# State-space steps of a hybrid block: inputs scaled once, whole-tile products with ScalarE placing the halves, one scan per tile

## The chip, the cores and the metric

The kernel runs on one core of a Trainium2 chip. The core has a matrix engine (TensorE, PE in the tables), a vector engine (VectorE, DVE), a scalar engine (ScalarE, ACT), a general engine (GpSimd, POOL) and a queue engine (SyncE, SP) that only issues transfers. They run side by side and wait for one another by semaphores; each takes its own instructions strictly in the order in which they were placed. The metric is the device time of one launch in microseconds (us).

## The reference, cut to what matters

The whole program is two transformer-like blocks, each with a mixture of experts. The change lies in one part of the first block, the state-space mix of 512 channels in 32 groups of 16, with 64 complex states for each group, over a sequence of 1024, once forwards and once backwards:

```python
def _ssm_direction(ug, a_re, a_im, log_dt, b_re, b_im, c_re, c_im, reverse):
    lam = lax.complex(a_re, a_im)
    dt = jnp.exp(log_dt)[:, None]
    a_bar = jnp.exp(lam * dt)
    b_bar = ((a_bar - 1.0) / lam)[..., None] * b_mat      # input matrix, scaled
    bu = jnp.einsum('blgc,gnc->blgn', ug, b_bar)
    _, h = lax.associative_scan(_scan_combine, (a, bu), axis=1, reverse=reverse)
    return jnp.einsum('blgn,gcn->blgc', h, c_mat).real

y = _ssm_direction(..., False) + _ssm_direction(..., True)
y = y + d_skip * u
```

In the same block 20 column blocks of a projection (`h @ w_in`, four for the Fourier part and 16 for the gates) don't depend on the state-space part.

## The kernel before, in words

The stage in question is the middle of `phase_a`. Two generators are run together there. `gates` has 20 column blocks of 128; each loads 512 KB of weights, splits them into a high and a low part (`split_hi_lo`: ScalarE copies the high part `sh`, line 55; VectorE subtracts for the low part `sl`, line 61), and multiplies twice 24 products of 128x512 into the PSUM tile `psg` (lines 210 to 212, helper `fm_block`; 960 products in all). ScalarE takes each finished `psg` into `go` (line 339). `ssm_steps` is the other one. The sequence of 1024 is cut into 128 blocks of 8 positions, the 32 groups into 4 lots `b`, with 2 directions `d`: 8 steps. What the two loops set is only the order in the program text. A list scheduler then fixes the order of the instructions on each engine when the program is built, with estimated durations; it places the rest of the program too.

A step has four pieces, and piece after piece is emitted a loop turn later than the one before, so that neighbouring steps overlap:
- `params1` scales the input matrix (`bbr`, `bbi`, a complex product `cmul` of 64 columns, lines 149 to 154), multiplies it with powers of the decay into `ptr` and `pti` (`cmul`, 512 columns), turns the output matrix by four products on TensorE (line 564, into `ct`), builds the block-diagonal `cbd` on GpSimd (lines 568 to 572), and forms `q`, whose real part stands in partitions 0 to 63 and whose imaginary part in 64 to 127 (lines 580 to 589). In `ptr` and the other parameter tiles the two halves of the partitions are instead two groups of channels, so real and imaginary results have to be placed half by half.
- `params2` builds rotation tables `ec`, `es` on GpSimd, and turns `ptr` and `pti` on TensorE (line 606), copied out by ScalarE into `pres` and `pims` (line 607). `ug_make` turns the inputs into `ug` (lines 623, 624).
- `scan` multiplies `ug` with `pres` and `pims` (line 634), rotates the result (lines 642 to 647, with two of the six operations on GpSimd), runs the recurrence as eight scans of 128 columns (line 651), rotates back (lines 661 to 667), and places the result in `st` by halves (lines 665, 670).
- `r_make` and `y_out` move a small convolution block through memory and form the output (lines 710, 712).

Ahead of the stage, `phase_a` reads and normalizes `x`, and projects the state-space inputs `us` (line 320 copies them out). `ssm_params` forms the decay powers, and loads `b_re`, `b_im`, `c_re`, `c_im`. A third generator, `ada_steps` (lines 1361 to 1388), forms a modulation vector out of large weights `w_ada`: 8 parts of it run beside the projection of `us`, and one goes with each call of `gates` from the 21st on. The rest of the program (the gated unit and the Fourier part, the first mixture of experts, the second block) follows in order.

Of the kernel before, what the change touches and what calls it, by code (L numbers as in the profile page):

```python
# [13 lines left out]
AF = mybir.ActivationFunctionType  # L14
OP = mybir.AluOpType
AX = mybir.AxisListType
P = 128
# [10 lines left out]
class Core:  # L28
# [6 lines left out]
    def sb(self, pool, shape, dt=FT, tag=None, bufs=None):  # L35
        self.n += 1
        kw = {"name": f"{tag or 't'}_{self.n}"}
        kw["tag"] = tag or kw["name"]
        if bufs is not None:
            kw["bufs"] = bufs  # L40
        return pool.tile(shape, dt, **kw)


def bcast(ap, shape):
    return ap.to_broadcast(shape)
# [102 lines left out]
def cmul(E, o_re, o_im, a_re, a_im, b_re, b_im, t1, t2):  # L148
    E.tensor_tensor(t1, a_re, b_re, op=OP.mult)
    E.tensor_tensor(t2, a_im, b_im, op=OP.mult)  # L150
    E.tensor_tensor(o_re, t1, t2, op=OP.subtract)
    E.tensor_tensor(t1, a_re, b_im, op=OP.mult)
    E.tensor_tensor(t2, a_im, b_re, op=OP.mult)
    E.tensor_tensor(o_im, t1, t2, op=OP.add)
# [275 lines left out]
def ssm_params(k, keep, pool, prm, T):  # L430
    nc = k.nc
    V, G, A, PE = nc.vector, nc.gpsimd, nc.scalar, nc.tensor
    sb = k.sb
# [8 lines left out]
    t1 = sb(pool, sh, tag="t1")  # L442
    t2 = sb(pool, sh, tag="t2")
# [24 lines left out]
    f_re = sb(keep, sh, tag="fre")  # L468
# [52 lines left out]
    for nm in ("re", "im"):  # L521
        tb["b_" + nm] = sb(keep, [P, 2, 16, 16], tag="b_" + nm)
        tb["c_" + nm] = sb(keep, [P, 2, 4, 64], tag="c_" + nm)
        for d in range(2):
            nc.sync.dma_start(out=tb["b_" + nm][:, d], in_=T["ssm_B_" + nm][0, d].rearrange("(q g) n c -> (g n) q c", g=2))
            nc.sync.dma_start(out=tb["c_" + nm][:, d],
                              in_=T["ssm_C_" + nm][0, d].rearrange("(b g) c n -> (g c) b n", b=4))
    return dict(**tb, pw_re=pw_re, pw_im=pw_im, f_re=f_re, f_im=f_im, r8=r8, er=er)


def ssm_steps(k, jit, pp, pr, us, ident, kd_d, T):
# [3 lines left out]

    def params1(b, d):
        br, bi = [pr[n][:, d, 4 * b:4 * b + 4] for n in ("b_re", "b_im")]
# [11 lines left out]
        b_re = sb(jit, [P, 4, 16], tag="bbr")  # L549
        b_im = sb(jit, [P, 4, 16], tag="bbi")  # L550
        fr = bcast(pr["f_re"][:, cols].unsqueeze(2), [P, 4, 16])
        fi = bcast(pr["f_im"][:, cols].unsqueeze(2), [P, 4, 16])
        cmul(V, b_re, b_im, br, bi, fr, fi, t1[:, :, 0, :], t2[:, :, 0, :])
# [7 lines left out]
        for g in range(2):  # L561
            pg = slice(64 * g, 64 * g + 64)
            for a, n in enumerate(("c_re", "c_im")):
                PE.matmul(ctp[pg, a * P:(a + 1) * P], pr[n][:, d, b, :], ident, start=True, stop=True)
            A.activation(ct[pg], ctp[pg, 0:256].rearrange("p (a q g c) -> p a q g c", a=2, q=4, g=2)[:, :, :, g, :],
                         AF.Copy)
        cbd = sb(jit, [P, 2, 4, 2, 16], tag="cbd")
        G.memset(cbd, 0.0)
        for g in range(2):
            pg = slice(64 * g, 64 * g + 64)  # L570
            G.tensor_copy(cbd[pg, 0, :, g, :], ct[pg, 0])
            G.tensor_scalar(cbd[pg, 1, :, g, :], ct[pg, 1], -1.0, None, op0=OP.mult)
# [5 lines left out]
        t1 = sb(jit, [P, 4, 8, 16], tag="p1")  # L578
        t2 = sb(jit, [P, 4, 8, 16], tag="p2")
        V.tensor_tensor(t1, cre, pre, op=OP.mult)  # L580
        V.tensor_tensor(t2, cim, pim, op=OP.mult)
        for g in range(2):
            pg = slice(64 * g, 64 * g + 64)
            V.tensor_tensor(q[0:64, :, g], t1[pg], t2[pg], op=OP.subtract)
        V.tensor_tensor(t1, cre, pim, op=OP.mult)
        V.tensor_tensor(t2, cim, pre, op=OP.mult)
        for g in range(2):
            pg = slice(64 * g, 64 * g + 64)
            V.scalar_tensor_tensor(q[64:128, :, g], t1[pg], -1.0, t2[pg], op0=OP.mult, op1=OP.subtract)
# [37 lines left out]
    def scan(b, d, pm, ug):  # L627
# [13 lines left out]
        t1, t2, t3, t4 = [sb(jit, [P, 4, 128], tag=f"t{i}", bufs=1) for i in (1, 2, 3, 4)]  # L641
# [5 lines left out]
        G.tensor_tensor(t3, t3, t4, op=OP.subtract)  # L647
        for w in (t1, t3):
            for i in range(4):
                ww = w[:, i, ::-1] if d else w[:, i, :]  # L650
                V.tensor_tensor_scan(ww, bcast(pr["r8"][:, c0 + i:c0 + i + 1], [P, 128]), ww, 0.0,
                                     op0=OP.mult, op1=OP.add)
# [9 lines left out]
        G.tensor_tensor(m2, hi_, es_, op=OP.mult)  # L662
        for g in range(2):
            pg = slice(64 * g, 64 * g + 64)
            V.tensor_tensor(st[0:64, :, g, o], t2[pg, :, 0:127], t4[pg, :, 0:127], op=OP.subtract)
        V.tensor_tensor(m1, hr_, es_, op=OP.mult)
        G.tensor_tensor(m2, hi_, ec_, op=OP.mult)
        for g in range(2):
            pg = slice(64 * g, 64 * g + 64)
            V.tensor_tensor(st[64:128, :, g, o], t2[pg, :, 0:127], t4[pg, :, 0:127], op=OP.add)  # L670
# [1986 lines left out]
```

## Time and profile before

| | |
|---|---|
| median of 3 runs | 3660.16 us (3659.49 to 3662.08) |
| the profiled execution | 3656.41 us |
| its span, first to last instruction | 3654.6 us |
| busy over the whole span: PE, DVE, ACT, POOL | 86%, 53%, 35%, 30% |

The busy shares of the whole span are an average over very different stages; what an edit in one stage is worth is read from that stage. The page's 40 slices have DVE at 9 tenths or more in some and at none in others. A duration that is shown for an instruction includes time in which it was held up after its start. "PEld" is the loading of weights into TensorE, beside its products.

### The profile page before, as it was taken

What the parts mean: (1) busy time and instruction counts of PE and PEld (TensorE: products, weight loads), DVE (VectorE), ACT (ScalarE), POOL (GpSimd) and SP (SyncE); (2) the same over time, 40 slices, a digit from 0 to 9 for tenths busy, and PEclk for the clock granted to TensorE, in tenths of its full rate; (3) what the DMA queues carried; (4) which work ended last, traced back from release to release, by engine and by line L of the source; (5) the groups of instructions that cost most, each with busy time, mean ns of one, the idle gap of its engine ahead of it and who ended that gap; (6) DMA issues with size and microseconds to landing.
All of it is one profiled execution on the core that took longest, in us unless ns stands there. A gap on an engine that the chain in (4) does not pass through costs nothing.

```text
span 3654.6 us, 54485 instructions
## 1 busy us (share of the span) xinstructions
PE 3141.0 (86%) x21219; PEld 2411.0 (66%) x21219; DVE 1937.4 (53%) x3265; ACT 1274.2 (35%) x2152; POOL 1114.6 (30%) x891
## 2 busy tenths in 40 slices
PE   6988989979888787777599988889999968999998
PEld 5777777965444444444287777667777966777776
DVE  7899566251100000000256766645676448999887
ACT  4212243210000000000143433326563227888775
POOL 1646243101111111111222344322232234445433
PEclk8998999989999999999899999989999988999999
DMA  7223436569999999999723344442225657999995
GB/s 199 75 69 92 140 137 213 200 255 416 417 412 414 411 414 406 409 412 402 269 64 110 84 116 121 119 144 84 80 84 148 200 189 258 360 358 365 356 331 180
DMA packets 489507, 869.03 MB, mean 238 GB/s; under 512 B 104767, under 2 KB 302223, under 8 KB 438816
## 3 DMA queue, kind: packets, MB, share of 16 engines
q1 hardware_dynamic: 445408, 790.27, 59.1%
q0 software_dynamic: 21552, 44.77, 4.9%
q10 hardware_dynamic: 22288, 30.48, 2.6%
q8 instruction: 169, 2.77, 0.3%
q14 instruction: 90, 0.74, 0.1%
HBM read 787.15 MB, written 94.93 MB: 241 GB/s over the span
## 4 chain that ended last, share of the span: by engine, by line
PE 25%; DVE 12%; DMA 6%; issue 4%; ACT 3%; POOL 1%; SPq 0%; POOLq 0%; ACTq 0%; DVEq 0%
DVE wl L61 4%; PE po L1889 2%; PE pt L1936 1%; ACT wh L55 1%; POOL wl L61 1%; DVE sil L1706 1%; DMA w<-in_w_gate 1%; DVE lt L1826 1%; PE ps L210 1%; PE ps L212 1%; PE ps L211 1%; DVE tm L1824 1%; PE sc L1917 1%; PE pst L66 1%; PE pst L67 1%
## 5 line engine op out<-in xcount | busy, mean ns | idle before, releaser
L1142 PE MATMUL gu<-w,xt 128*64 128x256 f32 x4096 | 526.4, 411 | 167.1 <-DMA w<-in_expert_w_gate 138.8
L1142 PEld LDWEIGHTS gu<-w,xt 128*64 128x64 f32 x4096 | 345.8, 148 | 363.3 <-issue 192.5
L61 DVE TENSOR_TENSOR wl<-w,wh 128x1024 fp32r<-128x1024 f32 x310 | 455.0, 1515 | 45.5 <-ACT wh L55 44.9
L55 ACT ACTIVATE wh<-w 128x1024 fp32r<-128x1024 f32 x412 | 419.5, 1058 | 108.7 <-PE pg L67 30.6
L61 POOL TENSOR_TENSOR wl<-w,wh 128x1024 fp32r<-128x1024 f32 x102 | 288.5, 2843 | 272.9 <-ACT wh L55 217.9
L1114 POOL DMA_INDIRECT xg<-x5d,si x64 | 67.2, 1050 | 730.2 <-PE xp L1125 655.3
L1154 ACT ACTIVATE h<-gu,icole 128x256 f32<-128x256 f32 x64 | 30.4, 474 | 710.3 <-PE gu L1142 710.3
L1127 DVE TENSOR_TENSOR xt<-xp,gcolp 128x512 f32<-128x512 f32 x64 | 44.2, 691 | 439.8 <-PE gu L1142 428.0
L1163 PE MATMUL y<-w,hts 128*64 128x512 f32 x1024 | 233.8, 597 | 21.7 <-issue 17.6
L1159 DVE COPY hts<-ht 128x256 f32<-128x256 f32 x64 | 27.2, 424 | 383.2 <-PE ht L1157 383.2
L210 PE MATMUL ps<-hth,wh 128*128 128x512 f32 x448 | 180.3, 403 | 1.4 <-DVE qkt L1623 1.4
L212 PE MATMUL ps<-hth,wl 128*128 128x512 f32 x448 | 178.6, 399 | 0.0
L211 PE MATMUL ps<-htl,wh 128*128 128x512 f32 x448 | 177.8, 397 | 0.0
L1163 PEld LDWEIGHTS y<-w,hts 128*64 128x64 f32 x1024 | 78.6, 136 | 133.1 <-issue 124.9
L65 PE MATMUL ps<-soh,mgh 128*128 128x256 f32 x512 | 150.3, 293 | 6.4 <-DVE xr L416 6.4
L67 PE MATMUL ps<-soh,mgl 128*128 128x256 f32 x512 | 146.0, 285 | 0.0
L66 PE MATMUL ps<-sol,mgh 128*128 128x256 f32 x512 | 145.9, 285 | 0.0
L210 PE MATMUL psg<-hth,sh 128*128 128x512 f32 x320 | 134.2, 419 | 5.7 <-ACT us L320 3.5
L1133 POOL DMA_INDIRECT x2d<-ys,si x64 | 101.4, 1584 | 120.9 <-DMA x2d<-ys,si 59.7
L212 PE MATMUL psg<-hth,sl 128*128 128x512 f32 x320 | 131.2, 410 | 5.1 <-DVE sl L61 5.1
L211 PE MATMUL psg<-htl,sh 128*128 128x512 f32 x320 | 130.5, 408 | 0.0
L66 PE MATMUL pu<-wl,xh 128*128 128x512 f32 x256 | 105.6, 412 | 26.4 <-POOL wl L61 16.1
(945 smaller groups left out, 7818.3 us busy)
## 6 DMA issues: line engine op xcount, KB each, us to landing
w<-in_expert_w_gate SPq DMA_DIRECT2D x128, 1024.0 KB, 21.6
w<-in_expert_w_up SPq DMA_DIRECT2D x128, 1024.0 KB, 20.9
w<-in_expert_w_down SPq DMA_DIRECT2D x128, 1024.0 KB, 21.2
w<-in_w_gate SPq DMA_DIRECT2D x64, 1024.0 KB, 8.9
w<-in_w_up SPq DMA_DIRECT2D x64, 1024.0 KB, 7.5
w<-in_w_down SPq DMA_DIRECT2D x64, 1024.0 KB, 8.4
w<-in_w_in SPq DMA_DIRECT2D x52, 512.0 KB, 4.1
w<-in_w_ada SPq DMA_DIRECT2D x48, 512.0 KB, 4.5
```

The lines of the kernel that those rows point to most:

```text
L55: nc.scalar.activation(hi, src, AF.Copy)
L61: e.tensor_tensor(lo, src, f32(hi), op=OP.subtract)
L65: nc.tensor.matmul(out, lh, rh, start=start, stop=False)
L66: nc.tensor.matmul(out, lh, rl, start=False, stop=False)
L67: nc.tensor.matmul(out, ll, rh, start=False, stop=stop)
L210: k.nc.tensor.matmul(ps, wh[:, kk, j:j + P], rh[:, kk, sl], start=st, stop=False)
L211: k.nc.tensor.matmul(ps, wh[:, kk, j:j + P], rl[:, kk, sl], start=False, stop=False)
L212: k.nc.tensor.matmul(ps, wl[:, kk, j:j + P], rh[:, kk, sl], start=False, stop=sp)
L1133: self.k.nc.gpsimd.indirect_dma_start(out=self.x_d.rearrange("t (o d) -> (t o) d", o=2), out_offset=ind(ix), in_=ys, in_offset=None, compu ...
L1142: last = PE.matmul(ps[64 * j:64 * j + 64, a, :], xt[:, kk % 4, kk // 4], ww[:, 256 * j:256 * j + 256], start=kk == 0, stop=kk == 7)
L1163: last = PE.matmul(py[64 * o:64 * o + 64, :], ht[:, i, 64 * j:64 * j + 64], wd[j][:, i, 512 * o:512 * o + 512], start=j + i == 0, stop=j + ...
L1889: PE.matmul(po[64 * j:64 * j + 64, 0, :], self.v[:, kt, 64 * (hp // 2):64 * (hp // 2) + 64], pts[j][:, kt, :], start=kt == 0, stop=kt == N ...
```

## The change

`b_re` and `b_im` now come into `ssm_params` as raw tiles from which one complex product of 512 columns forms the scaled matrices for all 8 steps. The two parts of the output matrix are loaded into one tile `c`, and turned by a single transpose; ScalarE writes `ct` and the block-diagonal `cbd` straight from PSUM, and the zeros of `cbd` are written once. The products for `q` and for `st` are formed as whole tiles of 128 partitions, and ScalarE copies each half to its place. The four scans of 128 columns of a tile become one scan of 512 columns, whose multiplier tile `rm` has a zero where a segment begins; ScalarE fills the other 127 columns of each segment in every step. The tile `t4` of `scan` now shares the buffer `p2` of `params1`.

```diff
@@ -518,13 +518,19 @@
                  w1[:, :, :n], w2[:, :, :n])
         er.append((t_re, t_im))
     tb = {}
-    for nm in ("re", "im"):
+    raw = {}
+    tb["c"] = sb(keep, [P, 2, 4, 2, 64], tag="c_tb")
+    for a, nm in enumerate(("re", "im")):
+        raw[nm] = sb(pool, [P, 2, 16, 16], tag="braw" + nm)
         tb["b_" + nm] = sb(keep, [P, 2, 16, 16], tag="b_" + nm)
-        tb["c_" + nm] = sb(keep, [P, 2, 4, 64], tag="c_" + nm)
         for d in range(2):
-            nc.sync.dma_start(out=tb["b_" + nm][:, d], in_=T["ssm_B_" + nm][0, d].rearrange("(q g) n c -> (g n) q c", g=2))
-            nc.sync.dma_start(out=tb["c_" + nm][:, d],
+            nc.sync.dma_start(out=raw[nm][:, d], in_=T["ssm_B_" + nm][0, d].rearrange("(q g) n c -> (g n) q c", g=2))
+            nc.sync.dma_start(out=tb["c"][:, d, :, a],
                               in_=T["ssm_C_" + nm][0, d].rearrange("(b g) c n -> (g c) b n", b=4))
+    fr, fi = [bcast(x.unsqueeze(2), [P, 32, 16]) for x in (f_re, f_im)]
+    flat = [x.rearrange("p d q c -> p (d q) c") for x in (tb["b_re"], tb["b_im"], raw["re"], raw["im"])]
+    w1, w2 = [sb(pool, [P, 32, 16], tag=f"ew0{x}w") for x in "ri"]
+    cmul(V, *flat, fr, fi, w1, w2)
     return dict(**tb, pw_re=pw_re, pw_im=pw_im, f_re=f_re, f_im=f_im, r8=r8, er=er)
 
 
@@ -533,8 +539,13 @@
     V, G, A, PE = nc.vector, nc.gpsimd, nc.scalar, nc.tensor
     sb = k.sb
 
+    cbd = sb(jit, [P, 2, 4, 2, 16], tag="cbd")
+    rm = sb(jit, [P, 513], tag="rm")
+    for x in (cbd, rm):
+        G.memset(x, 0.0)
+
     def params1(b, d):
-        br, bi = [pr[n][:, d, 4 * b:4 * b + 4] for n in ("b_re", "b_im")]
+        b_re, b_im = [pr[n][:, d, 4 * b:4 * b + 4] for n in ("b_re", "b_im")]
         c0 = 16 * d + 4 * b
         cols = slice(c0, c0 + 4)
 
@@ -546,11 +557,6 @@
 
         t1 = sb(jit, [P, 4, 8, 16], tag="p1")
         t2 = sb(jit, [P, 4, 8, 16], tag="p2")
-        b_re = sb(jit, [P, 4, 16], tag="bbr")
-        b_im = sb(jit, [P, 4, 16], tag="bbi")
-        fr = bcast(pr["f_re"][:, cols].unsqueeze(2), [P, 4, 16])
-        fi = bcast(pr["f_im"][:, cols].unsqueeze(2), [P, 4, 16])
-        cmul(V, b_re, b_im, br, bi, fr, fi, t1[:, :, 0, :], t2[:, :, 0, :])
         ptr_ = sb(jit, [P, 4, 8, 16], tag="ptr")
         pti = sb(jit, [P, 4, 8, 16], tag="pti")
         bre = bcast(b_re.unsqueeze(2), [P, 4, 8, 16])
@@ -558,35 +564,31 @@
         cmul(V, ptr_, pti, bre, bim, pwv(pr["pw_re"], 0, 8, d == 0), pwv(pr["pw_im"], 0, 8, d == 0), t1, t2)
         ctp = sb(pp, [P, 512], tag="pss")
         ct = sb(jit, [P, 2, 4, 16], tag="ct")
-        for g in range(2):
-            pg = slice(64 * g, 64 * g + 64)
-            for a, n in enumerate(("c_re", "c_im")):
-                PE.matmul(ctp[pg, a * P:(a + 1) * P], pr[n][:, d, b, :], ident, start=True, stop=True)
-            A.activation(ct[pg], ctp[pg, 0:256].rearrange("p (a q g c) -> p a q g c", a=2, q=4, g=2)[:, :, :, g, :],
-                         AF.Copy)
-        cbd = sb(jit, [P, 2, 4, 2, 16], tag="cbd")
-        G.memset(cbd, 0.0)
-        for g in range(2):
-            pg = slice(64 * g, 64 * g + 64)
-            G.tensor_copy(cbd[pg, 0, :, g, :], ct[pg, 0])
-            G.tensor_scalar(cbd[pg, 1, :, g, :], ct[pg, 1], -1.0, None, op0=OP.mult)
+        PE.transpose(ctp[:, 0:P], pr["c"][:, d, b].rearrange("p a n -> p (a n)"), ident)
+        for a in range(2):
+            cv = ctp[64 * a:64 * a + 64, 0:P].rearrange("p (q g c) -> p q g c", q=4, g=2)
+            for g in range(2):
+                pg = slice(64 * g, 64 * g + 64)
+                A.activation(ct[pg, a], cv[:, :, g, :], AF.Copy)
+                A.activation(cbd[pg, a, :, g, :], cv[:, :, g, :], AF.Copy, scale=-1.0 if a else 1.0)
         q = sb(jit, [P, 4, 2, 8, 16], tag="q", bufs=4)
         cre = bcast(ct[:, 0].unsqueeze(2), [P, 4, 8, 16])
         cim = bcast(ct[:, 1].unsqueeze(2), [P, 4, 8, 16])
         pre = pwv(pr["pw_re"], 1, 9, d == 0)
         pim = pwv(pr["pw_im"], 1, 9, d == 0)
-        t1 = sb(jit, [P, 4, 8, 16], tag="p1")
         t2 = sb(jit, [P, 4, 8, 16], tag="p2")
-        V.tensor_tensor(t1, cre, pre, op=OP.mult)
+        q1 = sb(jit, [P, 4, 8, 16], tag="p1")
+        q2 = sb(jit, [P, 4, 8, 16], tag="p3")
+        V.tensor_tensor(q1, cre, pre, op=OP.mult)
         V.tensor_tensor(t2, cim, pim, op=OP.mult)
+        V.tensor_tensor(q1, q1, t2, op=OP.subtract)
+        V.tensor_tensor(q2, cre, pim, op=OP.mult)
+        V.tensor_tensor(t2, cim, pre, op=OP.mult)
+        V.tensor_tensor(q2, q2, t2, op=OP.add)
         for g in range(2):
             pg = slice(64 * g, 64 * g + 64)
-            V.tensor_tensor(q[0:64, :, g], t1[pg], t2[pg], op=OP.subtract)
-        V.tensor_tensor(t1, cre, pim, op=OP.mult)
-        V.tensor_tensor(t2, cim, pre, op=OP.mult)
-        for g in range(2):
-            pg = slice(64 * g, 64 * g + 64)
-            V.scalar_tensor_tensor(q[64:128, :, g], t1[pg], -1.0, t2[pg], op0=OP.mult, op1=OP.subtract)
+            A.activation(q[0:64, :, g], q1[pg], AF.Copy)
+            A.activation(q[64:128, :, g], q2[pg], AF.Copy, scale=-1.0)
         return dict(q=q, ptr=ptr_, pti=pti, cbd=cbd, cols=cols)
 
     def params2(b, d, p1):
@@ -638,18 +640,22 @@
         ec, es = pm["ec"], pm["es"]
         if d:
             ec, es = ec[:, :, ::-1], es[:, :, ::-1]
-        t1, t2, t3, t4 = [sb(jit, [P, 4, 128], tag=f"t{i}", bufs=1) for i in (1, 2, 3, 4)]
+        t1, t2, t3 = [sb(jit, [P, 4, 128], tag=f"t{i}", bufs=1) for i in (1, 2, 3)]
+        t4 = sb(jit, [P, 4, 8, 16], tag="p2").rearrange("p q a b -> p q (a b)")
         V.tensor_tensor(t1, vr3, ec, op=OP.mult)
         V.tensor_tensor(t2, vi3, es, op=OP.mult)
         G.tensor_tensor(t1, t1, t2, op=OP.add)
         V.tensor_tensor(t3, vi3, ec, op=OP.mult)
         V.tensor_tensor(t4, vr3, es, op=OP.mult)
         G.tensor_tensor(t3, t3, t4, op=OP.subtract)
+        A.activation(rm[:, 0:512].rearrange("p (q j) -> p q j", q=4)[:, :, 1:128],
+                     bcast(pr["r8"][:, c0:c0 + 4].unsqueeze(2), [P, 4, 127]), AF.Copy)
         for w in (t1, t3):
-            for i in range(4):
-                ww = w[:, i, ::-1] if d else w[:, i, :]
-                V.tensor_tensor_scan(ww, bcast(pr["r8"][:, c0 + i:c0 + i + 1], [P, 128]), ww, 0.0,
-                                     op0=OP.mult, op1=OP.add)
+            ww = w.rearrange("p q j -> p (q j)")
+            if d:
+                V.tensor_tensor_scan(ww[:, ::-1], rm[:, 512:0:-1], ww[:, ::-1], 0.0, op0=OP.mult, op1=OP.add)
+            else:
+                V.tensor_tensor_scan(ww, rm[:, 0:512], ww, 0.0, op0=OP.mult, op1=OP.add)
         st = sb(jit, [P, 4, 2, 128], tag="st", bufs=3)
         if d == 0:
             a, o, z = slice(0, 127), slice(1, 128), slice(0, 1)
@@ -660,14 +666,14 @@
         m1, m2 = t2[:, :, 0:127], t4[:, :, 0:127]
         V.tensor_tensor(m1, hr_, ec_, op=OP.mult)
         G.tensor_tensor(m2, hi_, es_, op=OP.mult)
+        V.tensor_tensor(m1, m1, m2, op=OP.subtract)
+        V.tensor_tensor(hr_, hr_, es_, op=OP.mult)
+        G.tensor_tensor(hi_, hi_, ec_, op=OP.mult)
+        V.tensor_tensor(hr_, hr_, hi_, op=OP.add)
         for g in range(2):
             pg = slice(64 * g, 64 * g + 64)
-            V.tensor_tensor(st[0:64, :, g, o], t2[pg, :, 0:127], t4[pg, :, 0:127], op=OP.subtract)
-        V.tensor_tensor(m1, hr_, es_, op=OP.mult)
-        G.tensor_tensor(m2, hi_, ec_, op=OP.mult)
-        for g in range(2):
-            pg = slice(64 * g, 64 * g + 64)
-            V.tensor_tensor(st[64:128, :, g, o], t2[pg, :, 0:127], t4[pg, :, 0:127], op=OP.add)
+            A.activation(st[0:64, :, g, o], m1[pg], AF.Copy)
+            A.activation(st[64:128, :, g, o], hr_[pg], AF.Copy)
         return st
 
     def r_make(b, pm):
```

What stands on the engines is decided by the scheduler, so a few pieces of its order follow. The list calls a scan SCALAR_TENSOR_TENSOR, and leaves out the number in names such as `t1` and `p2`.

On DVE before, in the middle of the third step's `scan` (lines 651 to 670) with `params1` of the next steps between (585 to 589, 149 to 154):

```order
L584 TENSOR_TENSOR q_2011<-p_311_2012,p_312_2013 64x4x128 x2
L651 SCALAR_TENSOR_TENSOR t_317_2068<-r_125_768,t_317_2068 128x128 x4
L585 TENSOR_TENSOR p_311_2012<-ct_1998,pwim_726 128x512
L586 TENSOR_TENSOR p_312_2013<-ct_1998,pwre_725 128x512
L651 SCALAR_TENSOR_TENSOR t_319_2070<-r_125_768,t_319_2070 128x128 x4
L661 TENSOR_TENSOR t_318_2069<-t_317_2068,ec_1897 128x4x127
L589 SCALAR_TENSOR_TENSOR q_2011<-p_311_2012,p_312_2013 64x4x128 x2
L665 TENSOR_TENSOR st_2086<-t_318_2069,t_320_2071 64x4x127 x2
L149 TENSOR_TENSOR p_349_2287<-b_re_930,fre_751 128x4x16
L150 TENSOR_TENSOR p_350_2288<-b_im_936,fim_752 128x4x16
L666 TENSOR_TENSOR t_318_2069<-t_317_2068,es_1898 128x4x127
```

The same place in the change, where 658 is a scan, 667 to 672 rotate back, 587 ends the products for `q`, and 149 and 150 begin the next `params1`:

```order
L658 SCALAR_TENSOR_TENSOR t_314_2043<-rm_1295,t_314_2043 128x512
L587 TENSOR_TENSOR p_309_1986<-p_309_1986,p_307_1984 128x512
L149 TENSOR_TENSOR p_346_2259<-b_re_932,pwre_725 128x512
L667 TENSOR_TENSOR t_315_2044<-t_314_2043,ec_1880 128x4x127
L649 TENSOR_TENSOR p_317_2046<-pvr_2025,es_1881 128x512
L670 TENSOR_TENSOR t_314_2043<-t_314_2043,es_1881 128x4x127
L658 SCALAR_TENSOR_TENSOR t_316_2045<-rm_1295,t_316_2045 128x512
L669 TENSOR_TENSOR t_315_2044<-t_315_2044,p_317_2046 128x4x127
L150 TENSOR_TENSOR p_347_2260<-b_im_938,pwim_726 128x512
L672 TENSOR_TENSOR t_314_2043<-t_314_2043,t_316_2045 128x4x127
```

The half-tile writes into `q` and `st` are gone from DVE, and line 669 stands one row behind the second scan; its second operand is made by GpSimd out of that scan (line 668).

On ACT before, a stretch with the copies for one step (565 and 607) between the gates' own copies (55 and 339):

```order
L565 ACTIVATE ct_1332<-pss_1331 64x128
L55 ACTIVATE sh_1617<-w_1619 128x1024
L339 ACTIVATE go_1390<-psg_1391 128x512
L607 ACTIVATE pres_1428<-pss_1430 128x512
L607 ACTIVATE pims_1429<-pss_1436 128x512
L339 ACTIVATE go_1472<-psg_1473 128x512
```

ACT in the change, two steps on (590, 591 place `q`; 675, 676 place `st`; 609 fills `pres`, `pims`):

```order
L675 ACTIVATE st_1599<-t_234_1587 64x4x127 x2
L676 ACTIVATE st_1599<-t_233_1586 64x4x127 x2
L55 ACTIVATE sh_2068<-w_2070 128x1024
L339 ACTIVATE go_1852<-psg_1853 128x512
L609 ACTIVATE pres_1890<-pss_1892 128x512
L339 ACTIVATE go_1934<-psg_1935 128x512
L590 ACTIVATE q_1761<-p_266_1763 64x4x128 x2
L609 ACTIVATE pims_1891<-pss_1898 128x512
L591 ACTIVATE q_1761<-p_267_1764 64x4x128 x2
```

The gates' copies 55 and 339 now stand behind copies that wait for results of DVE.

On SP, the difference at the start of the program; the loads of the output matrix stay ahead of the weights `w`, and those of `b` move (in the change they come behind the third pair of `w_ada` loads):

```order
 L182 DMA w_220<-in_w_in 128x8x128
-L525 DMA b_re_930<-in_ssm_B_re 128x16x16
-L526 DMA c_re_931<-in_ssm_C_re 128x4x64
-L525 DMA b_re_930<-in_ssm_B_re 128x16x16
-L526 DMA c_re_931<-in_ssm_C_re 128x4x64
-L525 DMA b_im_936<-in_ssm_B_im 128x16x16
-L526 DMA c_im_937<-in_ssm_C_im 128x4x64
-L525 DMA b_im_936<-in_ssm_B_im 128x16x16
-L526 DMA c_im_937<-in_ssm_C_im 128x4x64
+L528 DMA c_tb_930<-in_ssm_C_re 128x4x64 x2
+L528 DMA c_tb_930<-in_ssm_C_im 128x4x64 x2
 L182 DMA w_311<-in_w_in 128x8x128
```

Eight loads are now four ahead of the first block's weights, and four others stand later on the same queue.

## Rows read from the trace of the kernel before

**Rows 1.** Busy time by stretch (us): PE, PEld, DVE, ACT, POOL, clock share, DMA, GB/s.
```profile
109.40:467.00 357.60, 322.95 (x1740) 266.09 (x1740) 281.27 (x388) 78.23 (x145) 167.46 (x174) 0.92 0.31 92
136.80:376.00 239.20, 211.04 (x1212) 175.12 (x1211) 227.66 (x303) 50.93 (x96) 134.52 (x133) 0.91 0.25 73
```

**Rows 2.** Line 606 alone: durations (ns), first and last start (us).
```profile
L606 PE MATMUL pss<-ident,ptr x32: 271/272/446, 136.8 to 375.9; 128*128 128x128 f32 x32
```

**Rows 3.** What PE waited for from 109.4 to 467: us in total, times, longest.
```profile
PE pvr L634 <- ACT ug L624: 12.1, 2, 8.8
PE pss L606 <- DVE ptr L151: 6.3, 1, 6.3
PE psg L212 <- DVE sl L61: 5.1, 2, 4.6
...
PE psg L210 <- ACT us L320: 3.5, 1, 3.5
```

**Rows 4.** Busy time by stretch, as in Rows 1, two short ones.
```profile
180.00:190.00 10.00, 2.78 (x13) 1.82 (x11) 9.75 (x11) 2.25 (x3) 5.41 (x6) 0.72 0.15 44
430.00:460.00 30.00, 29.83 (x140) 24.28 (x139) 10.34 (x20) 8.61 (x17) 4.43 (x6) 1.00 0.49 149
```

**Rows 5.** DVE's groups from 120 to 380: count, busy us, mean ns, idle before.
```profile
L651 DVE TENSOR_TENSOR_SCAN t<-r,t 128x128 f32<-128x128 f32 x56 | 20.7, 431 | 1.9 <-POOL t L644 1.7
L584 DVE TENSOR_TENSOR q<-p,p 64x512 f32<-64x512 f32 x16 | 19.7, 1230 | 0.1
L670 DVE TENSOR_TENSOR st<-t,t 64x508 f32<-64x508 f32 x13 | 19.4, 1492 | 0.4
...
L589 DVE SCALAR_TENSOR_TENSOR q<-p,p 64x512 f32<-64x512 f32 x16 | 16.6, 1039 | 0.4
L665 DVE TENSOR_TENSOR st<-t,t 64x508 f32<-64x508 f32 x14 | 9.5, 679 | 0.2
...
L152 DVE TENSOR_TENSOR p<-b_re,fim 128x64 f32<-128x64 f32 x8 | 7.5, 943 | 0.2
...
L151 DVE TENSOR_TENSOR ptr<-p,p 128x512 f32<-128x512 f32 x8 | 7.2, 902 | 0.4
...
L149 DVE TENSOR_TENSOR p<-b_re,fre 128x64 f32<-128x64 f32 x8 | 2.5, 311 | 0.1
```

**Rows 6.** The timeline of DVE and POOL: start us, us, instruction, count.
```profile
161.83 1.29 POOL L644 TENSOR_TENSOR t<-t,t 128x512 f32<-128x512 f32 x1 [6.97 <-DVE t L643]
162.19 3.17 DVE L584 TENSOR_TENSOR q<-p,p 64x512 f32<-64x512 f32 x2
...
167.87 1.36 DVE L651 TENSOR_TENSOR_SCAN t<-r,t 128x128 f32<-128x128 f32 x4
...
192.36 1.38 DVE L584 TENSOR_TENSOR q<-p,p 64x512 f32<-64x512 f32 x2
```

**Rows 7.** POOL's groups and one of ACT's, 120 to 380, columns as in Rows 5.
```profile
L662 POOL TENSOR_TENSOR t<-t,es 128x508 f32<-128x508 f32 x7 | 12.3, 1753 | 36.7 <-DVE t L651 34.5 <-ACT ug L624 2.3
...
L572 POOL TENSOR_SCALAR cbd<-ct 64x64 f32<-64x64 f32 x16 | 9.3, 579 | 0.7
...
L607 ACT ACTIVATE pres<-pss 128x512 f32<-128x512 f32 x7 | 4.1, 592 | 6.2 <-PE pss L606 6.2
```

**Rows 8.** PE's timeline around line 564: start us, us, instruction, count.
```profile
122.21 0.39 PE L212 MATMUL psg<-hth,sl 128*128 128x512 f32 x1
122.53 0.43 PE L564 MATMUL pss<-ident,c_re 128*64 128x128 f32 x2
...
123.11 0.50 PE L210 MATMUL psg<-hth,sh 128*128 128x512 f32 x1
```

**Rows 9.** ACT's timeline at the end of the projection of `us`.
```profile
107.79 1.30 ACT L1365 ACTIVATE w<-w,cs__64_338 128x256 f32<-128x256 f32 x3 [6.34 <-DMA w<-in_w_ada]
109.00 0.36 ACT L320 ACTIVATE us<-ps 128x256 f32<-128x256 f32 x1
```

**Rows 10.** Busy time by stretch, as in Rows 1, while `b` and `c` are loaded.
```profile
14.00:24.00 10.00, 5.33 (x21) 3.76 (x21) 9.59 (x29) 8.92 (x15) 0.00 (x0) 1.00 1.04 178
```

## The prediction, on record before the change was run

> **What bounds the kernel now.** I read the page's slices first, to find the place of the change: all of it lies in the first eighth of the span. Then busy time by stretch. The stage in which the gates' products and the state-space steps run together lasts from 109.4 to 467.0, 357.6 us. PE is busy for 323.0 of these and idle for 34.6, DVE is busy for 281.3, and the granted clock is 0.92 [rows 1]. The eight steps themselves can be timed by the turning of `ptr` on PE (line 606): from the first at 136.8 to the last at 375.9, seven intervals in 239 us, 34.2 us a step [rows 2]. In that stretch DVE is busy for 227.7 of 239.2 us (95%), PE for 211.0 (88%), GpSimd for 134.5 (56%) [rows 1]. So a step is paced by DVE, at 32.5 us busy of 34.2; behind the steps, at 430 to 460, PE alone is full and DVE a third busy [rows 4].
>
> The waits of PE say the same with one detour. 12.1 us go to the copy of `ug`, 6.3 to `ptr`, 5.1 to a weight split [rows 3]. The first is a ScalarE copy, but ScalarE is busy for only 78 of 357.6 us [rows 1]: such a copy is late because something ahead of it in ScalarE's order waited for DVE or for a buffer that DVE had yet to release. [...]
>
> **The change, part by part.** *DVE loses*, per step, by the means of its groups [rows 5]: the six 64-column products, whose means run from 0.31 to 0.94 (32.8 us for the 48, 4.1 a step); the half-tile writes of `q`, 2 x 1.23 + 2 x 1.04 = 4.5; those of `st`, 2 x 0.68 + 2 x 1.49 = 4.3; eight scans of 128, 8 x 0.43 = 3.4. Together 16.4 us.
>
> *DVE gains* four whole-tile operations at 0.90, that of `ptr`, which has the same shape [rows 5]: 3.6 us. And two scans of 512 columns, which no row shows. Below, a scan can't well beat a plain operation of 512 columns, 0.69 (half of the pair at 192.36, a half tile but the same columns); above, four scans of 128 as they stand, 4 x 0.43 = 1.7 [rows 5]. Undisturbed, four take 1.36 [rows 6], with four starts instead of one; I take 1.2, so 2.4 a step. Net: 16.4 - 6.0 = 10.4 us less, and DVE needs 32.5 - 10.4 = 22.1 us a step (bounds 21.1 and 23.1 for the scan).
>
> Half tiles are the right thing to remove, since they cost as many columns as whole ones: the pair of line 584 takes 1.38 us alone, and 3.17 with a GpSimd operation starting at 161.83 just ahead of it [rows 6]. [...]
>
> *ScalarE gains* about eight copies of 512 columns in half tiles and one for `rm`, bounded above by a whole copy at 0.59 [rows 7]: nine, 5.3 us, and some 2 us of small ones for `ct` and `cbd`. That is 58 us on top of 78 in the stage: no bound by itself.
>
> *GpSimd loses* 32 small operations into `cbd`, at most 0.58 each [rows 7]: 2.3 us a step, of 134.5 / 7 = 19.2.
>
> *PE loses* four products per step. One group's pair of products, with the changeover, holds up the gates by 123.11 - 122.21 = 0.90 us where a product of the gates takes about 0.23 from start to start: 0.67 each, 1.3 a step [rows 8]. One transpose at about 0.25 stays: 1.1 less.
>
> What is then PE's own need? In the stretch, 211.0 us busy. At a mean clock of 0.91, 43 of the 239 us were at the low one; if all 28 us of idling were among them, 15 busy us ran at half speed and 7.5 would be saved, if none, 21.5 [rows 1]. I take 15. Then (211 - 15) / 7 - 1.1 = 26.9 us a step (bounds 26.0 and 28.0). DVE, at 22.1, drops below PE; PE becomes the bound, and the step goes from 34.2 to at least 26.9, a gain of 51 us in seven.
>
> Not all of it comes. The second and third step stand denser in PE's order than before (61 and 43 gate products between their turns instead of 66 and 72), and 43 products at 0.23 with a step's own some 8 us are 18 us, less than DVE needs; I take 5 us of waiting there. Waits for `ada_steps` and for weights remain; with the lower clock behind each I take 8. So 51 - 13 = 38. New waits on DVE: the last operand of line 669 is made by GpSimd out of the second scan, 1.75 us [rows 7], with one operation of 0.7 between; about 1 us a step, within DVE's slack of 4.8. Behind 669 on DVE stands the next `params1`, for which PE waits. The shared buffer `p2` costs nothing as long as that is so, since DVE takes its users in order anyway.
>
> At the edges: another step or so of PE work saved behind the stretch, 2 us. At 109.4 PE waits 3.5 us for the last `us` copy [rows 3], which stands behind a part of `ada_steps` whose weights are late [rows 9]; in the change one part fewer is ahead of it: -3.5. Against that, the loads of `b` move into the projection, where `ada_steps` waits for its weights; with those of `c` they are most of what fills the transfer engines (share 1.04, at only 178 GB/s) for 10 us at 14 to 24 [rows 10], so perhaps half is passed on, and half of that is hidden: 0 to 6, I take 3. The new six whole-tile products ahead of the stage, 6 x 0.9 = 5.4 us, lie on a DVE that is not yet full; 0, at most 5.4.
>
> Sum: -38 - 2 - 3.5 + 3 = -40 us on the profiled execution's 3656.4, so 3616. The median of the runs shown is 3.75 us above that execution; forecast 3620. All that follows the stage is taken to move up unchanged.
>
> **The rivals.** *DVE and GpSimd stay the bound* (0.20). If they shut each other out, a step needs their own times one after the other. What is saved in own time is less: eight half tiles at 0.69, eight scans at 0.34, six small ones at 0.31 at most, 2.3 of GpSimd, against four whole tiles at 0.69 and 2.4 of scans: 7.2 us, so 34.2 falls to 27.0, level with PE, and each wait of a step's chain then shows. With 1.75 for line 668 and as much for a weight split behind ScalarE's new copies, 30.5 a step: a gain of 26 and 2 at the edges, 3632. [...]
>
> *Slower, by ScalarE's order* (0.10). `sh` and `go` now stand behind copies that wait for DVE. `psg` has two buffers, some 5.5 us of products each; where a placement is late by more, PE stops, twice a step, at 16 places. It decides at 40 / 16 = 2.5 us a place; at 3.5 the time would be 3676. The longest such stop now is 8.8 us [rows 3], but ScalarE is idle for most of the stage.
>
> *No change* (0.08). The scheduler also reorders parts of later stages, and `b`'s loads come late; if these give back all but a few us: about 3656. Nothing in the rows prices that order; I keep 10 us of the range for it.
>
> *All of it* (0.07). Every idle us of the stage comes back, the clock with it (by the same halving as above, 20 us at 0.92 of 357.6), and 8 x 1.1 of PE's own work: 34.6 + 20 + 9 = 64, 3596.
>
> **How the numbers follow.** The forecast has 0.55, by itself 3608 to 3632. Taking in the second bound and the fuller gain, and 10 us for later stages, the range is 3602 to 3650. A measurement of this kernel tells about 0.2%, 7 us, from no change. Faster 0.82, same 0.08, slower 0.10.
>
> **What would show it.** Right: line 606's counterpart from first to last in about 201 us, DVE busy there for about 155, PE idle below 15 us in the whole stage, its clock at 0.95 or above, and the stage some 38 us shorter; scans of about 1.2 us. Wrong: DVE at 95% again (second bound), PE waiting for `go` or `sh` (ScalarE's order), a projection longer than 65 us (`b`'s loads), or stages after it that are not as long as before.

## The result, and the profile after

The changed kernel takes 3623.18 us (median of 4 runs, 3620.81 to 3627.10), the one before 3661.12 us beside it: ratio 0.9897, 95% interval 0.9886 to 0.9909. The forecast was 3620, 3602 to 3650. The profiled execution of after took 3623.40 us with a span of 3621.6, so 33.0 us of span are to be explained; the rest of the 38 us is that the profiled execution of before was 4.7 us below its median.

Busy time by stretch, after: start to first `psg`, stage, steps (first to last `ptr` on line 608), and what follows. Columns as in [rows 1].

```profile
0.00:102.90 102.90, 68.99 (x464) 64.33 (x464) 82.07 (x304) 43.88 (x81) 25.66 (x47) 0.90 0.70 190
102.90:435.60 332.70, 308.07 (x1684) 255.85 (x1685) 232.62 (x269) 128.46 (x267) 165.45 (x149) 0.95 0.35 103
138.40:349.20 210.80, 190.31 (x1112) 157.76 (x1110) 182.91 (x190) 93.50 (x200) 126.41 (x98) 0.94 0.29 82
435.60:3700.00 3264.40, 2749.40 (x19018) 2075.51 (x19016) 1576.01 (x2571) 1148.37 (x1924) 915.72 (x658) 0.95 0.69 250
```

Set against before, whose stage is taken here to the end of its last gate product at 466.6 and whose steps are taken to the first turn of the last one at 375.5: the stage starts 6.5 us earlier and is 24.5 shorter, and what follows it takes 2.0 less. Within the stage the seven intervals shrink from 239 to 211 us, 34.1 to 30.1 a step, while 8 us more lie ahead of them (149 gate products where 102 were; 47 fewer, 523 for 570, lie in the steps) and 5 us fewer behind. PE idles for 24.6 us of the stage instead of 34.6. DVE is busy for 182.9 of 210.8 us (87%) in the steps, 26.1 a step where 22.1 was forecast. GpSimd is at 126.4, little below the 134.5 of before.

What the operations of DVE cost now, 120 to 380, columns as in [rows 5]:

```profile
L656 DVE TENSOR_TENSOR_SCAN t<-rm,t 128x512 f32<-128x512 f32 x8 | 12.2, 1524 | 5.5 <-POOL t L647 4.1 <-POOL t L650 1.4
L150 DVE TENSOR_TENSOR p<-b_im,pwim 128x512 f32<-128x512 f32 x8 | 11.2, 1401 | 0.2
L672 DVE TENSOR_TENSOR t<-t,t 128x508 f32<-128x508 f32 x7 | 11.0, 1568 | 0.0
L658 DVE TENSOR_TENSOR_SCAN t<-rm,t 128x512 f32<-128x512 f32 x8 | 10.8, 1348 | 1.2 <-POOL t L650 1.2
...
L669 DVE TENSOR_TENSOR t<-t,p 128x508 f32<-128x508 f32 x7 | 6.9, 990 | 5.1 <-POOL p L668 5.1
...
L587 DVE TENSOR_TENSOR p<-p,p 128x512 f32<-128x512 f32 x8 | 6.3, 789 | 0.0
...
L646 DVE TENSOR_TENSOR t<-pvi,es 128x512 f32<-128x512 f32 x8 | 5.5, 682 | 0.0
```

Products of one shape have means from 0.68 to 1.57 us; those with an input in PSUM (line 646) keep 0.68. The timeline shows why. First DVE, then POOL, as in [rows 6]:

```profile
200.07 1.55 DVE L672 TENSOR_TENSOR t<-t,t 128x508 f32<-128x508 f32 x1
201.54 1.55 DVE L151 TENSOR_TENSOR ptr<-p,p 128x512 f32<-128x512 f32 x1
203.13 1.64 DVE L152 TENSOR_TENSOR p<-b_re,pwim 128x512 f32<-128x512 f32 x1
204.69 1.55 DVE L153 TENSOR_TENSOR p<-b_im,pwre 128x512 f32<-128x512 f32 x1
206.17 1.55 DVE L585 TENSOR_TENSOR p<-ct,pwim 128x512 f32<-128x512 f32 x1
207.64 0.68 DVE L154 TENSOR_TENSOR pti<-p,p 128x512 f32<-128x512 f32 x1
208.24 0.68 DVE L645 TENSOR_TENSOR t<-pvr,ec 128x512 f32<-128x512 f32 x1
208.84 0.68 DVE L582 TENSOR_TENSOR p<-ct,pwre 128x512 f32<-128x512 f32 x1
```

```profile
201.04 1.51 POOL L153 TENSOR_TENSOR u<-er0i,er3r 128x512 f32<-128x512 f32 x1
202.63 1.59 POOL L154 TENSOR_TENSOR es<-u,u 128x512 f32<-128x512 f32 x1
204.30 1.40 POOL L149 TENSOR_TENSOR u<-er0r,er3r 128x512 f32<-128x512 f32 x1
205.66 1.51 POOL L150 TENSOR_TENSOR u<-er0i,er3i 128x512 f32<-128x512 f32 x1
210.87 1.29 POOL L647 TENSOR_TENSOR t<-t,t 128x512 f32<-128x512 f32 x1 [3.70 <-DVE t L646]
```

As long as GpSimd works on the rotation tables, the two engines go in step, about 1.5 us for one operation of each; when GpSimd stops at 207.2, DVE's products follow each other every 0.60 us.

What PE waited for in the stage, columns as in [rows 3]:

```profile
PE pss L608 <- ACT us L720: 9.1, 5, 3.0
PE pss L608 <- DVE ptr L151: 4.1, 1, 4.1
PE pss L625 <- ACT ks L616: 3.5, 1, 3.5
PE psg L210 <- ACT sh L55: 3.4, 2, 1.7
PE psg L210 <- ACT us L320: 2.9, 1, 2.9
```

The largest is for a ScalarE copy again: `us` (line 720) stands on ScalarE behind the placements of `q` and `st`, which wait for DVE.

### The profile page after: what moved, and what is told of

It is laid out like the page before. It is cut to its first block, busy times and chain, and to the rows that moved or that the text cites. A ratio compares the mean times of both kernels' runs of the same rounds, so it can differ in the third digit from the quotient of the medians.

```text
span 3621.6 us, 54283 instructions
## 1 busy us (share of the span) xinstructions
PE 3126.5 (86%) x21163; PEld 2395.7 (66%) x21163; DVE 1890.7 (52%) x3143; ACT 1320.7 (36%) x2272; POOL 1106.8 (31%) x853
## 5 line engine op out<-in xcount | busy, mean ns | idle before, releaser
L1165 DVE COPY hts<-ht 128x256 f32<-128x256 f32 x64 | 27.2, 424 | 382.4 <-PE ht L1163 382.4
L66 PE MATMUL pg<-wl,xh 128*128 128x512 f32 x256 | 106.7, 417 | 19.2 <-DVE wl L61 19.0
```

The source lines that it names most:

```text
L66: nc.tensor.matmul(out, lh, rl, start=False, stop=False)
```

## The experiments

Theory 1: DVE and GpSimd shut each other out, and what is missing of the stage's gain is lost there. Theory 2: ScalarE's order makes PE wait. Theory 3: PE's own need bounds the stage already. Theory 4 (for what moving operations gains): it was the hand-overs between engines, not exclusion. The chips of these runs were slower for all (before: 3668 to 3670 us), so kernels are compared by their ratio to the before that ran beside them; 0.001 is 3.7 us. The changed kernel's is 0.9897, from the result above; it did not run again beside them. A difference of two ratios is uncertain by some 6 us.

| kernel | ratio to before | 95% interval |
|---|---|---|
| rotation tables once | 0.9832 | 0.9819 to 0.9846 |
| four operations to VectorE | 0.9842 | 0.9829 to 0.9855 |
| all ten to VectorE | 0.9810 | 0.9797 to 0.9823 |
| `us` copies to VectorE | 0.9888 | 0.9873 to 0.9903 |
| before + scan | 0.9984 | 0.9973 to 0.9994 |
| before + whole tiles | 0.9929 | 0.9916 to 0.9941 |
| before + inputs | 0.9920 | 0.9907 to 0.9933 |
| all ten, idle GpSimd given reads | 0.9897 | 0.9883 to 0.9911 |
| all ten, idle GpSimd given memsets | 0.9819 | 0.9803 to 0.9834 |
| before, its ten to VectorE | 0.9899 | 0.9881 to 0.9916 |
| all ten, rotation tables once | 0.9800 | 0.9785 to 0.9815 |

### GpSimd's work left out, or moved

Rotation tables once (changed kernel):

```diff
-        cmul(G, o_re, o_im, a_re, a_im, b_re, b_im, u1, u2)
+        if b == 0:
+            cmul(G, o_re, o_im, a_re, a_im, b_re, b_im, u1, u2)
```

> The changed kernel, with the rotation tables ec and es formed for the first step of each direction alone and used again by the other six: 36 of the 48 GpSimd products of line 644's cmul are left out, and the output differs for that. Theory 1 (VectorE and GpSimd shut each other out: in the changed kernel a 512-column product with both inputs in SBUF lasts 0.60 us from start to start beside an idle GpSimd and about 1.55 beside a working one): VectorE busy between the first and last line 608 falls from 183 us to about 150, PE's idle time there from 20.5 to below 10, the step from 30.2 to 28 or less, the whole kernel to 3600 to 3606 us, 17 to 23 below the changed kernel. Theory 2 (PE waits because ScalarE's copies stand in an order that makes us copies queue behind q placements; GpSimd has nothing to do with it): no more than 5 us gained. Theory 3 (PE's own 27.2 us a step bound the stage and the rest is the schedule's noise): no more than 5 us either way.

Four operations to VectorE (lines 647, 650, 668, 671), and the six of the tables too:

```diff
-        G.tensor_tensor(t1, t1, t2, op=OP.add)
+        V.tensor_tensor(t1, t1, t2, op=OP.add)
...
-        cmul(G, o_re, o_im, a_re, a_im, b_re, b_im, u1, u2)
+        cmul(V, o_re, o_im, a_re, a_im, b_re, b_im, u1, u2)
```

> The changed kernel with the four GpSimd operations of the scan (lines 647, 650, 668, 671) on VectorE. Theory 1 (mutual exclusion): VectorE gains 4 x 0.60 us a step and loses four stretches in which it runs at 1.55 instead of 0.60, and the chain from the products over the scan to st gets shorter by two or three hand-overs; the step falls by 1 to 2 us, the kernel by 7 to 14 us, to 3609 to 3616. Without exclusion, VectorE is just loaded with 2.4 to 2.8 us a step more on its 26.2: the step grows, 5 to 15 us slower than the changed kernel. Theory 2 (ScalarE's order): between -4 and +4 us.

> As the one with four operations moved, and the six products of the rotation tables on VectorE too, so that GpSimd is nearly idle in the steps. Theory 1: ten operations of 0.60 us come to VectorE, 6 us a step, and every operation of it runs undisturbed: some 30 products at 0.60, two scans at 1.15 and the weight splits are 25 to 27 us a step, as busy as in the changed kernel, with no hand-overs; 3605 to 3622 us. Without exclusion: 26.2 + 6 = 32 us a step, above PE's 27.2, the kernel 10 to 25 us slower than the changed one, 3633 to 3648.

All three gained, by 24, 20 and 32 us over the changed kernel; the first about at the upper end of theory 1, the other two beyond it, and without exclusion the last two should have lost. The steps with the rotation tables formed once:

```profile
137.30:325.90 188.60, 180.52 (x1112) 151.31 (x1111) 155.12 (x190) 94.89 (x203) 74.64 (x63) 0.98 0.34 94
```

The same 190 operations of DVE as in the changed kernel take 155.1 us instead of 182.9, with GpSimd busy for 74.6 instead of 126.4. The busy time of stretches with all ten on VectorE (stage, then steps):

```profile
101.80:405.70 303.90, 296.57 (x1685) 248.30 (x1685) 220.46 (x351) 128.77 (x267) 52.90 (x69) 0.98 0.39 113
138.40:322.80 184.40, 179.73 (x1106) 151.85 (x1105) 170.05 (x264) 95.47 (x202) 25.51 (x26) 0.97 0.33 93
```

DVE runs 264 operations in 170.1 us there, the changed kernel's DVE 190 in 182.9: more operations and less time. PE idles for 7 us of the stage, at a clock of 0.98, and a step takes 26.3 us. This version beats both kernels: 3598.26 us, beside 3667.69 of before.

### The `us` copies

```diff
-            A.activation(us[:, 8 * b + 4 * h:8 * b + 4 * h + 4].rearrange("p g s c -> p (g s c)"), ps, AF.Copy)
+            V.tensor_copy(us[:, 8 * b + 4 * h:8 * b + 4 * h + 4].rearrange("p g s c -> p (g s c)"), ps)
```

> The changed kernel with the us copies of line 720 (out of PSUM, two for every second step) on VectorE instead of ScalarE. Theory 2 (ScalarE's order): PE's 9.1 us of waiting for these copies behind the q placements go, and with them the half-speed clock behind each of five stops: 10 to 18 us faster than the changed kernel. Theory 1 (VectorE is late because of GpSimd, and the copies are only where that shows): PE then waits for something else that VectorE makes; -5 to +5 us.

No difference beyond the intervals. PE waits 8.7 us for the same copies on their new engine:

```profile
PE pss L608 <- DVE us L720: 8.7, 4, 3.1
PE pss L625 <- ACT ks L616: 5.5, 1, 5.5
PE pss L608 <- DVE ptr L151: 4.1, 1, 4.1
```

So theory 2 falls for these copies: their place was where a late DVE showed, not the cause. The version with all ten on VectorE agrees: its ScalarE has the same copies to make, PE has no wait for line 720 left, and its largest in the stage is 2.8 us in four, for `go`.

### The parts alone

Each is one part of the change put on the kernel before, with its lines of the diff ahead of the prediction; the first two also share `p2` as there. The core of each:

```diff
+                V.tensor_tensor_scan(ww, rm[:, 0:512], ww, 0.0, op0=OP.mult, op1=OP.add)
...
+            A.activation(st[0:64, :, g, o], m1[pg], AF.Copy)
...
+    cmul(V, *flat, fr, fi, w1, w2)
```

> The kernel before with one part of the change: the four scans of a tile as one of 512 columns with rm (filled by ScalarE), t4 in the buffer of p2. By the means of before, eight scans at 0.43 against two at 1.35 (measured in the changed kernel): 0.7 us of VectorE a step, 5 us faster than before if VectorE paces it. By own times under mutual exclusion, 8 x 0.34 against 2 x 1.15: 0.4 a step, 3 us. The copy of rm behind a late ScalarE could cost: +2. So 3653 to 3661, near before's 3661.

> The kernel before with one part of the change: q and st formed as whole tiles, their halves placed by ScalarE. If VectorE alone paces the step (forecast's terms): 8.8 us of half tiles against four at 0.90, 5.2 us a step, up to 36 us faster. By own times under mutual exclusion: eight half tiles at 0.60 against four, 2.4 a step, 17 us faster. If the placements by ScalarE hurt (rival of its order): slower than before or no gain.

> The kernel before with one part of the change: the inputs scaled once, c loaded into one tile and turned by one transpose, cbd filled by ScalarE. Forecast's terms: 4.1 us of VectorE, 2.3 of GpSimd and 1.1 of PE a step. Under mutual exclusion the own times count one after the other, 1.9 + 2.3 = 4.2 us, 29 us faster in seven steps; with VectorE alone, the same 4.1 or 29 us. If the earlier start of the stage (102.9 us in the changed kernel against 109.4) comes with this part, it shows here and not in the other two parts.

The scan gave 6 us, the whole tiles 26, the inputs 29: 61 in sum, the three together 38. Why they don't add up is not shown. In the profiled executions the stages are shorter than before's by 4.8, 19.5 and 8.7 us, 33.0 in sum, and by 24.5 with all three, so some 8 of the missing 23 us lie there; for the rest, behind the stage, there is no profile of before from the chip of these three. That PE's own need stops the sum does not fit: PE idles for 24.6 us in the stage of the changed kernel and for 22.3 in that with the whole tiles alone. The whole tiles came between the two prices given. That the inputs came to just the 29 us of their price is luck: the price was for the steps alone, and in the profiled execution the whole stage gave 8.7 and the earlier start 7.4. The earlier start belongs to the inputs: the stage begins at 102.0 there, at 109.2 and 109.6 in the other two. Busy time ahead of the stage, in the kernel with the inputs alone, then in that with the scan alone:

```profile
0.00:102.00 102.00, 69.26 (x465) 63.66 (x465) 80.15 (x301) 43.86 (x81) 24.90 (x47) 0.93 0.69 191
```

```profile
0.00:109.20 109.20, 73.07 (x466) 66.49 (x466) 81.57 (x306) 45.32 (x84) 32.04 (x60) 0.97 0.68 191
```

Against the scan alone about half is idle time of PE (32.7 and 36.1 us), half busy time of as many instructions; against the whole tiles alone, idle time is 5.6 us of 7.6. With the inputs formed once, five parts of `ada_steps` instead of six pass PE ahead of the stage, and its waits for GpSimd's sums of them fall from 8.5 to 0.9 us; but other waits grow by more than half of that, the one for the first `x` from 2.2 to 5.7. Why just this order comes out 7 us shorter stays open; no run changes it alone.

### Reads against writes on GpSimd

Both start from the version with all ten on VectorE, and give GpSimd work for which nobody waits (`u2` shares `p2`'s buffer to make room):

```diff
+        gd = sb(jit, [P, 4, 128], tag="gd").rearrange("p q (a b) -> p q a b", b=8)
+        for x, y in ((a_re, b_re), (a_im, b_im), (a_re, b_im)) * 2:
+            G.tensor_tensor(gd, x, y, op=OP.mult)
```

> The version with all ten operations on VectorE (3598 beside a before of 3668, ratio 0.981), and in each step six GpSimd products of 512 columns, both inputs in SBUF, into a tile that nobody reads (u2 shares the buffer of p2 to make room). No instruction waits for them. Theory 1 (mutual exclusion): VectorE's two-input products beside them go from 0.60 to about 1.55, its busy time between first and last line 608 from 170 to 190 or more, and the step from 26.4 to 28 to 30: 10 to 25 us slower than without them. Theory 4 (moving the operations helped because the chain over the scan lost its hand-overs between two engines and GpSimd's slower 1.3 us, not by exclusion): 0 to 3 us slower.

```diff
+        gd = sb(jit, [P, 4, 128], tag="gd")
+        for _ in range(18):
+            G.memset(gd, 0.0)
```

> As the one with six GpSimd products, but with 18 GpSimd memsets of 512 columns, which read nothing and keep GpSimd as busy (0.45 to 0.54 us each, 8 to 10 us a step). If it is the reading of SBUF by both engines that shuts one out, VectorE's products stay at 0.60 and the time at that of the version without them, within 4 us. If any GpSimd work does it, 10 to 25 us slower, as with the products.

The reads cost 32 us, all that the moving had gained; the memsets 3 us, within the intervals. The steps of the kernel with reads, then of that with memsets:

```profile
135.30:349.80 214.50, 191.86 (x1109) 160.42 (x1108) 209.60 (x264) 95.40 (x202) 81.58 (x70) 0.90 0.29 82
```

```profile
139.30:321.80 182.50, 179.53 (x1109) 152.19 (x1108) 175.41 (x263) 95.03 (x201) 89.74 (x162) 0.97 0.34 96
```

GpSimd is busy for 82 and 90 us; DVE, with 264 and 263 operations, for 210 and 175. The timeline of DVE in the kernel with reads, while GpSimd multiplies (up to 209.5) and after, and in that with memsets, 15 of which fill 194.5 to 203.2:

```profile
207.06 1.55 DVE L582 TENSOR_TENSOR p<-ct,pwre 128x512 f32<-128x512 f32 x1
208.54 1.55 DVE L583 TENSOR_TENSOR p<-ct,pwim 128x512 f32<-128x512 f32 x1
210.01 0.68 DVE L674 TENSOR_TENSOR t<-t,es 128x508 f32<-128x508 f32 x1
210.61 0.68 DVE L584 TENSOR_TENSOR p<-p,p 128x512 f32<-128x512 f32 x1
```

```profile
196.87 0.68 DVE L151 TENSOR_TENSOR ptr<-p,p 128x512 f32<-128x512 f32 x1
197.58 0.69 DVE L152 TENSOR_TENSOR p<-b_re,pwim 128x512 f32<-128x512 f32 x1
```

Theory 4 isn't needed for the 32 us: no chain goes through `gd`. What hand-overs added to the 20 us of the four moved operations stays open.

### The kernel before with its ten on VectorE, and one more cut

The ten operations are those of the kernel before (lines 644, 647, 662, 667 and its `cmul` on G):

```diff
-        G.tensor_tensor(m2, hi_, ec_, op=OP.mult)
+        V.tensor_tensor(m2, hi_, ec_, op=OP.mult)
```

> The kernel before, without the change, and with its ten GpSimd operations of 512 columns a step (lines 644, 647, 662, 667 and the six of the rotation tables) on VectorE. Theory 1: before, VectorE is busy 32.5 of 34.2 us a step, much of it in exclusion; its operations of 512 columns at 0.60 (20 with the half tiles counted one by one, and ten more), eight scans at 0.34, six small ones at 0.1 to 0.3, and the splits make 27 to 30 us: 15 to 35 us faster than before, most of what the change gives, 3633 to 3653 beside a before of 3668. Without exclusion: VectorE 32.5 + 6 to 7 us a step, 39 us: 35 us or more slower.

> The version with all ten operations on VectorE, with the rotation tables formed for the first step of each direction alone (36 products left out, the output differs for it). VectorE loses 3.6 us of its 24.3 a step. If PE's own need bounds that version, the time stays within 5 us of it (ratio 0.981 to before); if VectorE still paces it, 10 us or more are gained.

Moving ten operations, and nothing of the change, gave 0.9899, more than was expected and as much as the whole change with 0.9897. Its steps:

```profile
142.10:339.80 197.70, 191.64 (x1188) 161.74 (x1187) 192.58 (x359) 51.52 (x96) 38.98 (x61) 0.98 0.31 88
```

DVE is busy for 27.5 us of a 28.2 us step there, at the lower end of what was expected. In the version with all ten moved, leaving out 36 more products of DVE changed nothing that the intervals tell (0.9800 against 0.9810), though DVE's busy time in the steps fell from 170 to 151 us:

```profile
139.50:320.30 180.80, 177.97 (x1106) 150.81 (x1105) 151.44 (x228) 95.52 (x202) 17.42 (x26) 0.98 0.34 97
```

PE is busy for 178.0 of 180.8 us: there PE bounds the stage, which theory 3 claimed too early.

## Why the prediction came out as it did

**What bounds the kernel.** DVE as the pacer of the steps was read rightly, its 32.5 us a step as its need was not. Two pairs of runs separate the two. Seventy operations of 0.60 us, 42 us, came to DVE with the ten; without them the kernel before would need 192.6 - 42 = 151 us in seven steps, and was busy for 227: 76 us, a third, was exclusion. For the changed kernel, 170.1 - 42 = 128 and 182.9: 55 us (both estimates from those rows; the stretches differ a little, so that DVE has 56 operations more in the one pair and 74 in the other, not 70).

A second estimate counts every DVE operation of the steps at its interval from start to start when GpSimd doesn't hold it up (0.60 us for whole tiles, 0.69 for half tiles, 0.32 and 1.12 for scans of 128 and 512 columns, 1.14 for a weight split, 0.13 to 0.39 for the small ones). It gives 150 us of own time and 77 of exclusion before, and 120 and 62 for the changed kernel. By the same count exclusion is 65 to 70 us in the kernels with one part alone, 43 with four operations moved, 35 with the rotation tables once, 5 with all ten moved, and then 45 with GpSimd's reads and 11 with its memsets.

**The step that failed** is the net of 10.4 us of DVE a step. It gave back each removed operation at its mean of before, and kept the others at theirs. But how long DVE is shut out goes mostly with GpSimd's reading (264 operations took DVE 209.6 us beside added products of GpSimd, and 263 took 175.4 beside added memsets), and the change leaves all ten of its large operations; when fewer DVE operations stand beside them, those that stand there carry most of it (55 of 76 us by the first estimate). Measured: DVE's busy time fell from 227 to 183 us, 6.3 a step. Of that, 151 - 128 = 23 us, 3.3 a step, is own time by the first estimate and 76 - 55 = 21, 3.0 a step, exclusion; by the second it is 4.2 and 2.1. The four whole-tile operations at 0.90 cost 0.79 to 1.57 each. The scan at 1.2 was right by itself (1.21 beside an idle GpSimd) and 1.35 to 1.52 in place.

**PE's own need** was forecast as 26.9 a step and was 190.3 / 7 = 27.2, some of it at the low clock (0.94 granted on the mean); with all ten moved it was 25.7 (0.97). That the low clock is half of the full one stood in the forecast without a row; the trace of before shows it, with gate products every 0.43 us instead of 0.23 (columns as in [rows 1]):

```profile
185.00:194.00 9.00, 5.09 (x16) 4.08 (x17) 8.78 (x14) 1.19 (x2) 1.09 (x2) 0.50 0.37 107
```

The 8 us for waits "with the lower clock behind each" were an estimate that no run shows: behind stops of 4.1 and 3.0 us of the changed kernel the clock was at 0.50 and at 1.00.

The nearness of 26.9 to 27.2 flatters the forecast, which was made for the 570 gate products of before: 523 and 518 lay in these steps, and the others at 0.23 would add 1.5 and 1.7 a step. With DVE at 26.1, two engines are about level, and whatever is late on DVE shows on PE: 20.5 us of idling in the steps against 13 for all residual waits. "PE becomes the bound" was half true of the change and wholly of the version with all ten on VectorE, where the stage's predicted marks (idle below 15 us, clock above 0.95) are met.

**The rivals.** The first one, that DVE and GpSimd stay the bound, had the mechanism and nearly the step: 30.5 forecast, 30.1 measured. The forecast's 28.7 was further off. The runs show the mechanism, and that it goes with GpSimd's reading: in the timelines above a product of DVE took 1.55 us beside GpSimd's products and 0.68 beside its memsets. The rival's 3632 missed by 9 us and the forecast by 3, since the rival had nothing for the earlier start either; and its sign, DVE at 95% again, did not come (87%). Of ScalarE's order, the `us` copies cost no net time, and PE's waits for `sh` and `go`, the sign that was named, are 3.7 us in the stage after 2.1 before; no run moved these. ScalarE's busy time in the stage grew by 50 us where 58 was said. The wait of line 669 is 5.1 us in seven steps, close to the one a step given.

**The edges.** The loads of `b` cost nothing that shows (forecast +3), and the stage started 6.5 us earlier, where -0.5 was the net. Both belong to the inputs; the cause is open. The wait for the last `us` copy, said to vanish, stands at 2.9. What follows the stage moved up almost unchanged (2.0 us less).

**The sum.** In spans, 40 us were forecast and 33 came: the stage with its edges behind gave 24.5 instead of 40, the start 6 more, the rest 2 more. That 3623 lies so near 3620 is in good part luck: it comes of the earlier start and of the low profiled execution of before, for which 3.75 us were added, not of the model of DVE. Of the signs of being right (steps in 201 us, DVE busy for 155, idle below 15, clock 0.95, a stage 38 us shorter, scans of 1.2) only the clock came as said; measured were 211, 183, 24.6, 0.95, 24.5, and 1.35 to 1.52.

## What to carry to other kernels

Here DVE and GpSimd were both busy with operands in SBUF, and DVE's busy time was no measure of its need (182.9 us in the steps, 128 by the first estimate): look in the timeline for one shape at two durations before pricing what an edit removes. An operation taken off DVE onto GpSimd may cost DVE more than doing it: here a pair took 1.5 us on the two engines and 1.2 on DVE alone. Try moving GpSimd's share over before reshaping the work; ten changed engine names were worth as much here as the whole change, and both together 70 us.

## What the runs showed of the hardware

DVE's products with two SBUF inputs and GpSimd's went in lockstep in the stretches shown, one of each per 1.47 to 1.6 us, for as long as both had work; products with one input in PSUM took 0.66 to 0.69 us throughout in the changed kernel, beside a working GpSimd too (0.68 for line 648 at 210.64, with line 647 on GpSimd from 210.87), and beside memsets of GpSimd (15 in 8.69 us, 0.53 each on the mean) DVE's products in that stretch kept 0.68 to 0.69.

Some short stops of PE cost more than their length. Behind its stop of 4.1 us that ended at 177.3 the granted clock of the changed kernel was 0.50 for 6 us, with gate products every 0.43 us instead of 0.23, and behind two stops of 1.6 and 1.9 us it was low again for some 3 us (0.57 from 217 to 221). It doesn't follow every stop: behind one of 3.0 us that ended at 287.1 the clock stayed full (1.00, last line), so the half-speed clock that was expected behind each of PE's five stops for `us` copies was too much:

```profile
172.00:177.00 5.00, 1.15 (x6) 0.61 (x4) 5.00 (x3) 1.88 (x3) 4.57 (x5) 0.94 0.02 3
177.00:183.00 6.00, 5.73 (x16) 4.70 (x17) 6.00 (x9) 1.61 (x3) 2.79 (x2) 0.50 0.41 111
214.00:217.00 3.00, 0.66 (x4) 0.42 (x4) 3.00 (x6) 2.27 (x5) 0.00 (x0) 1.00 0.00 0
217.00:221.00 4.00, 3.88 (x12) 3.22 (x13) 1.77 (x2) 0.69 (x2) 2.63 (x2) 0.57 0.00 0
287.00:293.00 6.00, 5.93 (x33) 5.13 (x33) 0.00 (x0) 2.27 (x6) 4.75 (x5) 1.00 0.12 44
```
